# The filler of the sample's attention: two products of each of eight gate pairs in place of two whole pairs

## The chip, the cores and the metric

The kernel runs on one core of a Trainium2 chip. Its time is the device time of one execution in microseconds (us); a measurement runs it several times and takes the median. The core has five engines that work side by side, each through its own list of instructions in a fixed order: TensorE (PE in the profile; its weight loads are PEld), VectorE (DVE), ScalarE (ACT), GpSimd (POOL) and SyncE (SP). SP issues every DMA transfer of this kernel. Engines wait for each other by semaphores. TensorE writes into PSUM, which has eight banks of 128 x 512 fp32 values here; the others read it from there.

## What is computed

One encoder layer, applied to two batches with the same weights: the prompt (512 tokens) and the sample (1024 tokens), 1024 channels each. Cut to what matters:

```python
h = rmsnorm(x, norm_g)
proj = h @ w_in                       # q, k, v, z of two branches; gates ga, gb (1024 wide each)
oa = neighbourhood_attention(qa, ka, va, rpb_a) * silu(za)
ob = window_gqa_attention(qb, kb, vb, t5_table, sink_b) * silu(zb)
merged = sigmoid(ga) * (oa @ w_o_a) + sigmoid(gb) * (ob @ w_o_b)
return x + merged @ w_out
```

The change concerns `ga` and `gb` of the sample: per branch eight blocks of 128 channels (m = 0 to 7), each the product of a 1024 x 128 weight block with h (1024 x 1024 tokens), then a sigmoid.

## The kernel before

**Stages.** The prompt goes first (attention, then the dense phase), then the sample (attention, then the dense phase). In attention, projections (line 761), scores (L934), softmax (L969, L978, L1002 to L1010), transposes (L1026), their split into two parts (L1032, L1037) and the product with v (L1063) alternate. A dense phase is: z pairs (8 blocks of silu(z) times the attention's result), gate pairs (16 blocks of g), the merge (`w_o` products times the sigmoids), and the output projection.

**Precision.** An operand is kept as a high part and a low part (`whi`, `wlo` for weights, `hh`, `hl` for h). `split` (L1163) makes them: ScalarE copies the high part (L1167), VectorE or GpSimd subtracts for the low part (L1172). `product` (L1276) multiplies one 512 x 128 weight block with 512 tokens: 4 steps k of 3 matmuls (L1284 to L1286), 12 matmuls, accumulated in one bank.

**Pairs.** Two neighbouring blocks of channels, two halves of the 1024 input channels and two halves of the tokens form a 2 x 2 by 2 x 2 block product. `pair_classic` makes it with eight products. `pair_strassen` (L1320) makes it with seven: four sums of the weights s1 to s4 (tiles `S`), four sums of h made ahead (`T`), and additions of the results on VectorE (`U`, `C`, L1340 to L1364). Its first two products use no sum at all: product 0 is weight block (0,0) with h block (0,0), product 1 is weight block (0,1) with h block (1,0). Product 0, copied to p1 (L1353), is added to product 1 for the result (0,0), the first channel block's first token half, and it also goes into u2, on which the other results build. Results pass a sigmoid (L1387) and are stored to `g_d` in DRAM (L1394), from where the merge loads them.

**The filler.** `fill_gates` (L1466) makes some gate blocks during attention. Its matmuls have their own weights (`fr` loaded, split to `fh` and `fl`, two buffers each) and their own bank `d`, of which there is one. A finished bank is copied to `fc`, one buffer, by ScalarE or VectorE (L1493), and stored without its sigmoid; the merge then applies the sigmoid in place (L1566). In the sample `FILL_S = 2` makes the last two pairs, branch b's blocks 4 to 7, in this way: per block two token halves, each two products in a row in bank d. The dense phase leaves those pairs out (L1518).

**Order.** All instructions are ordered ahead by a planner, `Flow.run`. It simulates the engines with assumed durations and lags, and gives a free engine the ready operation of the lowest priority number. In the sample's attention the priorities run from 100 to 148; the filler's matmuls and loads have 195, its splits and copies 110 (`soon`), the dense phase 200 and more (a z pair i has 200 + i, a gate pair i 204 + i, the merge 212 + m). So the filler's matmuls go where PE has nothing of attention ready, and its splits and copies ahead of most of attention. The order found is fixed: at run time an engine waits at its next instruction. Weights and tiles rotate through a few buffers, some strictly in turn: `raw` 4, `S` 3, `U` 4, `whi` and `wlo` 6 each of 6 blocks of 128 columns. The first z pair is a classic one; its first two outputs (48 matmuls) need nothing of attention's end, while the sums' products wait until attention's memory is given back (`opened`).

Of the kernel before, what the change touches and what calls it, by code (L numbers as in the profile page):

```python
# [24 lines left out]
ROTA = "ppxxxxxd"  # L25
FILL_P, FILL_S = 3, 2
SLACK = 1.1
# [13 lines left out]
P = 128  # L41
# [313 lines left out]
def encoder_kernel(  # L355
# [780 lines left out]
    def dense_phase(geo, hh, hl, h_ops, o_stores, exps_done, start, opened, tp, up, p0, p1, p2, x_t, y_t, classic, fill, after_gates=None, side=None):  # L1136
# [138 lines left out]

        def product(ps, ws, movs, prio, first, last, after=(), n=nh):  # L1276

            o = None
            for k, ((hi, lo, c, wops), (mh, ml, mops, mv)) in enumerate(zip(ws, movs)):

                def emit(e, k=k, hi=hi, lo=lo, c=c, mh=mh, ml=ml):
                    out = ps.t[:, :n]
                    cs = slice(c, c + P)
                    pe.matmul(out, hi.t[:, cs], mh(), start=first and k == 0, stop=False)  # L1284
                    pe.matmul(out, hi.t[:, cs], ml(), start=False, stop=False)  # L1285
                    pe.matmul(out, lo.t[:, cs], mh(), start=False, stop=last and k == len(ws) - 1)  # L1286
# [32 lines left out]

        def pair_strassen(srcs, post, prio, mov_h, mov_t, seed=None, last=False):  # L1320
            raw = {(m, i): load_raw(srcs[m][i], prio - 2) for m, i in ((0, 0), (1, 0), (1, 1), (0, 1))}
            s1, s2, s3, s4 = (tile_("S", 3, 512) for _ in range(4))
            for out, in0, in1, op in (
# [19 lines left out]
            def result(m, n, x, bank, op=ALU.add):  # L1343
# [122 lines left out]
        def fill_gates(prio):  # L1466


            done = {(k, n): [o for t in range(n * nh // P, (n + 1) * nh // P) for o in h_ops[t]] for k in range(KC) for n in halves}
            mov = blocks(done, nh)  # L1470
            soon = (100 if nt == NT_S else 0) + SOON - f.base
            for br, m in filled:
                his, los = ([f.value(wpool, [P, nh], F32R, tag, 2) for _ in range(2)] for tag in ("fh", "fl"))
                ws = []
                for j in range(2):
                    raw = f.value(wpool, [P, nh], F32, "fr", 2)
                    dma(
                        lambda raw=raw, src=w_g[m, 2 * br + j]: nc.sync.dma_start(raw.t, src), 262144, prio, new=[raw],
                        after=[f.begun[nt, 1 if nt == NT_P else 0]],
                    )  # L1480
                    hi, lo = his[j], los[j]
                    ops = split(
                        lambda hi=hi: hi.t, lambda lo=lo: lo.t, lambda raw=raw: raw.t, nh, soon, (hi, True), (lo, True), [raw],
                    )
                    ws.append([(hi, lo, q * P, ops) for q in range(4)])
                for n in halves:
                    ps = bank("d")
                    o = product(ps, ws[0], mov(0, n), prio, True, False)
                    h_reads.append(product(ps, ws[1], mov(1, n), prio, False, True, [o]))
                    v = f.value(wpool, [P, nh], F32, "fc", 1)  # L1490
                    f.op(
                        (("act", ACT_(nh, False)), ("dve", DVE_(nh))),
                        lambda e, v=v, ps=ps: act.activation(v.t, ps.t, AF.Copy) if e == "act" else dve.tensor_copy(v.t, ps.t),  # L1493
                        soon, new=[v], use=[ps], port=False,
                    )
                    store("g", (br, m, n), g_d[br, m, :, half[n]], v, nh, prio)

# [18 lines left out]
        for i in range(8):  # L1516
            br, m0 = i // 4, 2 * (i % 4)
            if (br, m0) in filled:  # L1518
                if side:
                    side(4 + i)  # L1520
                continue
            srcs = [[w_g[m, 2 * br + j] for j in range(2)] for m in (m0, m0 + 1)]
            post = lambda m, *a, br=br, m0=m0: post_gate(br, m0 + m, *a)
            if i >= 8 - g_classic:
                pair_classic(srcs, post, 4 + i, mov_c)
            else:
                pair_strassen(srcs, post, 4 + i, mov_h, mov_t)
            if side:
# [15 lines left out]
        for m in range(8):  # L1544
# [5 lines left out]
            for n in halves:  # L1550
                gs_ = []
                for br in range(2):
# [219 lines left out]
```

## Time and profile before

| | |
|---|---|
| Median of 3 runs | 1145.79 us (1144.96 to 1147.68) |
| Profiled execution, from the first to the last instruction | 1144.7 us |
| VectorE, ScalarE, GpSimd busy | 854.4, 644.9, 308.3 us |
| Moved by DMA | 159.86 MB, 140 GB/s on average |

The profile is of one execution. Busy time is the union of an engine's instructions; a matmul's row lasts longer than the distance to the next one, because they are pipelined. Rows of the view by stretches name a stretch in us, its length, the busy time of each engine with the number of instructions in brackets, the granted PE clock, the busy share of the DMA engines and GB/s. Rows of the timeline begin with start and duration in us. Rows of the view by tile give the least, median and greatest duration in ns and the first and last start in us. Rows of the view of waits give the sum in us, how often, and the longest. Rows of the groups by line give the count after x, then busy us, mean ns of one, and the idle time before it.

### The profile page before, as it was taken

To read this page: it belongs to the slowest core of one execution; us is meant where nothing else is said; L and a number is where in the kernel's file an instruction comes from. 1 tells how busy PE (TensorE), PEld (TensorE's weight loads), DVE (VectorE), ACT (ScalarE), POOL (GpSimd) and SP (SyncE) were. 2 spreads that over 40 slices of the span, in tenths; PEclk is the share of its full clock that TensorE was granted. 3 is DMA by queue.
4 is the path that set the end of the run, shared out by engine and by line. 5 is a ranking of instruction groups with operands and counts; after the bars stand their busy time and mean duration, and the time that the engine had idled before them with its cause. 6 is when DMAs were issued, how large, how long until landed. Compare 5 with 4: busy or idle time off the path is not lost.

```text
span 1144.7 us, 18482 instructions
## 1 busy us (share of the span) xinstructions
PE 1133.8 (99%) x6139; PEld 985.8 (86%) x6139; DVE 854.4 (75%) x1975; ACT 644.9 (56%) x1467; POOL 308.3 (27%) x413
## 2 busy tenths in 40 slices
PE   8999999999999999999999999999999999999998
PEld 6999988888888899999999888888888888788887
DVE  5888798497765468887778888865878755497984
ACT  5777987544433346665678988865534434343320
POOL 3653433000010054343333445330222210132110
PEclk9999999999999999999999999999999999999999
DMA  7854543488786422121221213226657335573072
GB/s 253 273 158 141 181 113 102 115 264 266 232 277 199 165 72 67 25 70 32 71 61 50 56 37 93 56 66 214 218 148 211 129 111 159 200 238 121 29 223 90
DMA packets 124705, 159.86 MB, mean 140 GB/s; under 512 B 28297, under 2 KB 66961, under 8 KB 124610
## 3 DMA queue, kind: packets, MB, share of 16 engines
q1 hardware_dynamic: 124610, 158.69, 45.4%
q8 instruction: 48, 0.79, 0.3%
q14 instruction: 47, 0.39, 0.1%
HBM read 121.93 MB, written 41.44 MB: 143 GB/s over the span
## 4 chain that ended last, share of the span: by engine, by line
PE 94%; DVE 2%; DMA 2%; ACT 1%; POOL 1%; issue 0%; SPq 0%; ACTq 0%; POOLq 0%
PE p L761 25%; PE x L1285 9%; PE x L1286 9%; PE x L1284 9%; PE x L1063 5%; PE x L1026 5%; PE x L934 4%; PE p L1284 4%; PE p L1285 4%; PE d L1284 4%; PE p L1286 4%; PE d L1286 4%; PE d L1285 4%; PE x L861 2%; DMA ot<-u_d 1%; DMA w<-in_w_att_dram 1%
## 5 line engine op out<-in xcount | busy, mean ns | idle before, releaser
L761 PE MATMUL p<-whi,hh 128*128 128x384 f32 x384 | 133.4, 348 | 0.0
L761 PE MATMUL p<-wlo,hh 128*128 128x384 f32 x384 | 133.1, 347 | 0.0
L761 PE MATMUL p<-whi,hl 128*128 128x384 f32 x384 | 132.4, 345 | 0.0
L978 ACT ACTIVATE sb<-sb,mx 128x384 f32<-128x384 f32 (+1 forms) x192 | 107.5, 563 | 22.4 <-DVE mx L969 22.2
L1167 ACT ACTIVATE whi<-raw 128x512 fp32r<-128x512 f32 (+1 forms) x140 | 81.1, 590 | 52.6 <-PE x L1285 26.2
L761 PE MATMUL p<-whi,hb 128*128 128x384 f32 x384 | 107.5, 347 | 0.0
L1172 POOL TENSOR_TENSOR wlo<-raw,whi 128x512 fp32r<-128x512 f32 (+1 forms) x29 | 40.9, 1413 | 242.4 <-ACT whi L1167 130.4
L1284 PE MATMUL x<-hh,whi 128*128 128x512 f32 x264 | 102.7, 389 | 0.0
L1285 PE MATMUL x<-hl,whi 128*128 128x512 f32 x264 | 102.7, 389 | 0.0
L1286 PE MATMUL x<-hh,wlo 128*128 128x512 f32 x264 | 102.7, 389 | 0.0
L1037 DVE TENSOR_TENSOR pp<-x,pp 128x512 fp32r<-128x512 f32 (+1 forms) x136 | 82.6, 638 | 18.9 <-ACT pp L1032 17.8
L1172 DVE TENSOR_TENSOR wlo<-raw,whi 128x512 fp32r<-128x512 f32 (+1 forms) x111 | 70.1, 645 | 30.5 <-ACT whi L1167 30.2
L1285 PE MATMUL x<-T,whi 128*128 128x512 f32 x224 | 87.5, 390 | 0.3 <-DVE T L1172 0.2
L1286 PE MATMUL x<-T,wlo 128*128 128x512 f32 x224 | 87.2, 389 | 0.0
L1284 PE MATMUL x<-T,whi 128*128 128x512 f32 x224 | 87.1, 389 | 0.0
L1032 ACT ACTIVATE pp<-x 128x512 fp32r<-128x512 f32 (+1 forms) x136 | 70.9, 560 | 22.8 <-PE x L1026 21.8
L799 POOL TENSOR_TENSOR rs_r<-rs_v,mhalf 128x4 f32<-128x4 f32 (+1 forms) x72 | 81.7, 1134 | 5.7
L1063 PE MATMUL x<-pp,v 128*128 128x256 f32 (+1 forms) x368 | 77.8, 324 | 0.8 <-DVE pp L1037 0.8
L792 POOL TENSOR_SCALAR rs_v<-ss 128x4 f32<-128x4 f32 (+1 forms) x72 | 26.2, 364 | 187.3 <-DVE ss L785 184.6
L761 PEld LDWEIGHTS p<-whi,hl 128*128 128x128 f32 x384 | 73.0, 190 | 1.3 <-issue 1.0
L761 PEld LDWEIGHTS p<-wlo,hh 128*128 128x128 f32 x384 | 73.0, 190 | 1.0 <-issue 0.5
L761 PEld LDWEIGHTS p<-whi,hh 128*128 128x128 f32 x384 | 73.0, 190 | 0.9 <-issue 0.5
(351 smaller groups left out, 2985.5 us busy)
## 6 DMA issues: line engine op xcount, KB each, us to landing
raw<-in_w_g_dram SPq DMA_DIRECT2D x76, 256.0 KB
w<-in_w_att_dram SPq DMA_DIRECT2D x46, 384.0 KB
ot<-o_d SPq DMA_DIRECT2D x36, 256.0 KB
g_d<-C SPq DMA_DIRECT2D x34, 256.0 KB
raw<-in_w_z_dram SPq DMA_DIRECT2D x32, 256.0 KB
raw<-in_w_out_dram SPq DMA_DIRECT2D x32, 256.0 KB
C<-g_d SPq DMA_DIRECT2D x24, 256.0 KB
out_dram<-C SPq DMA_DIRECT2D x23, 256.0 KB
```

Source lines behind the costliest of these rows:

```text
L761: pe.matmul(ps.t[:, :GW], part[u](k), mv.t[:, c], start=k == 0 and m == 0, stop=k == KC - 1 and m == 2,)
L799: lambda e: nc.gpsimd.tensor_tensor(r.t[:, :nn], rv.t[:, :nn], mhalf[:, :nn], op=ALU.pow),
L978: act.activation(sb.t[:, :width], sb.t[:, :width], AF.Exp, bias=mx.t[:, i : i + 1], scale=-1.0, accum_out=sm.t[:, i : i + 1],)
L1026: pe.transpose(pt.t[:, u * P : (u + 1) * P], sbs[i].t[:, c * P : (c + 1) * P], ident)
L1032: lambda e, pt=pt, pp=pp, nn=nn: act.activation(pp.t[:, 0, :nn], pt.t[:, :nn], AF.Copy),
L1037: lambda e, pt=pt, pp=pp, nn=nn: dve.tensor_tensor(pp.t[:, 1, :nn], pt.t[:, :nn], pp.t[:, 0, :nn].bitcast(F32), op=ALU.subtract),
L1063: pe.matmul(out(), v.t[:, vs], mv(), start=first, stop=last)
L1167: (("act", ACT_(n)),), lambda e: act.activation(hi(), src(), AF.Copy), prio,
L1172: lambda e: engines[e].tensor_tensor(lo(), src(), hi().bitcast(F32), op=ALU.subtract), prio,
L1284: pe.matmul(out, hi.t[:, cs], mh(), start=first and k == 0, stop=False)
L1285: pe.matmul(out, hi.t[:, cs], ml(), start=False, stop=False)
L1286: pe.matmul(out, lo.t[:, cs], mh(), start=False, stop=last and k == len(ws) - 1)
```

## The change

For the sample, all eight gate pairs now have a part in the filler (`FILL_S` is 8). Of each pair only the first channel block (`filled[::2]`) and only the two products without sums are made there: product 0 in bank d, whose copy is kept in DRAM (`p_d`) while the bank is not cleared; then, after that copy, product 1 on top of it in the same bank, whose copy is the result (0,0) and goes to `g_d`. The dense phase then makes every gate pair with five products; it loads product 0 into p1 instead of computing it, and neither makes nor stores the result (0,0). The merge applies its in-place sigmoid to the results (0,0) alone. The sums of weights, h and results are as before. The prompt takes none of this (`short`).

```diff
-FILL_P, FILL_S = 3, 2
+FILL_P, FILL_S = 3, 8
...
+        p_d = None if short else dpool.tile([2, 4, P, sn], F32, tag="p_d", name="p_d")
...
-        def pair_strassen(srcs, post, prio, mov_h, mov_t, seed=None, last=False):
+        def pair_strassen(srcs, post, prio, mov_h, mov_t, seed=None, last=False, kept=None):
...
-            w = weight_tiles([raw[0, 0], raw[0, 1], s2, s3, s1, raw[1, 1], s4], 6, prio - 0.5)
+            first = [] if kept else [raw[0, 0], raw[0, 1]]
+            w = weight_tiles([*first, s2, s3, s1, raw[1, 1], s4], 6, prio - 0.5)
+            w = [None] * (7 - len(w)) + w
...
-            a = mul(0, mov_h(0, 0))
-            f.op(
-                (("act", ACT_(sn)),), lambda e: act.activation(p1.t, a.t[:, :sn], AF.Copy), prio, new=[p1], use=[a]
-            )
-            result(0, 0, p1, mul(1, mov_h(1, 0)))
+            if kept:
+                src, after = kept
+                dma(lambda: nc.sync.dma_start(p1.t[:, :sn], src), 512 * sn, prio - 0.5, new=[p1], after=after)
+            else:
+                a = mul(0, mov_h(0, 0))
+                f.op(
+                    (("act", ACT_(sn)),), lambda e: act.activation(p1.t, a.t[:, :sn], AF.Copy), prio, new=[p1], use=[a]
+                )
+                result(0, 0, p1, mul(1, mov_h(1, 0)))
...
-            for br, m in filled:
+            for br, m in filled if short else filled[::2]:
...
-                for n in halves:
-                    ps = bank("d")
-                    o = product(ps, ws[0], mov(0, n), prio, True, False)
-                    h_reads.append(product(ps, ws[1], mov(1, n), prio, False, True, [o]))
...
+                for n in halves if short else (0,):
+                    ps = bank("d")
+                    o = product(ps, ws[0], mov(0, n), prio, True, not short)
+                    if not short:
+                        o = leave(ps, "p", (br, m), p_d[br, m // 2])
+                    h_reads.append(product(ps, ws[1], mov(1, n), prio, False, True, [o], again=not short))
+                    leave(ps, "g", (br, m, n), g_d[br, m, :, half[n]])
...
-            if (br, m0) in filled:
+            if (br, m0) in filled and short:
...
+                kept = (p_d[br, m0 // 2], stores["p", br, m0]) if (br, m0) in filled else None
+                pair_strassen(srcs, post, 4 + i, mov_h, mov_t, kept=kept)
...
-                    if (br, m) in filled:
+                    if (br, m) in filled and (short or (m % 2, n) == (0, 0)):
                         sigmoid(g, nh, prio, True)
```

`leave` is the copy to `fc` and the store, formerly written out in the loop. `again` tells the program's builder that the second product goes on in a bank whose group was closed.

More of the change, by code (lines that the diff above doesn't have):

```diff
@@ L1274, in weight_tiles, with product @@
             return out
-        def product(ps, ws, movs, prio, first, last, after=(), n=nh):
+        def product(ps, ws, movs, prio, first, last, after=(), n=nh, again=False):
             o = None
@@ L1283, in emit @@
                     cs = slice(c, c + P)
-                    pe.matmul(out, hi.t[:, cs], mh(), start=first and k == 0, stop=False)
-                    pe.matmul(out, hi.t[:, cs], ml(), start=False, stop=False)
-                    pe.matmul(out, lo.t[:, cs], mh(), start=False, stop=last and k == len(ws) - 1)
+                    more = {"skip_group_check": True} if again else {}
+                    pe.matmul(out, hi.t[:, cs], mh(), start=first and k == 0, stop=False, **more)
+                    pe.matmul(out, hi.t[:, cs], ml(), start=False, stop=False, **more)
+                    pe.matmul(out, lo.t[:, cs], mh(), start=False, stop=last and k == len(ws) - 1, **more)
                 kw = {"new": [ps]} if first and k == 0 else {"into": [ps]}
@@ L1485, in fill_gates, with leave @@
                     ws.append([(hi, lo, q * P, ops) for q in range(4)])
-                for n in halves:
-                    ps = bank("d")
-                    o = product(ps, ws[0], mov(0, n), prio, True, False)
-                    h_reads.append(product(ps, ws[1], mov(1, n), prio, False, True, [o]))
+                def leave(ps, kind, key, dst):
                     v = f.value(wpool, [P, nh], F32, "fc", 1)
-                    f.op(
+                    o = f.op(
                         (("act", ACT_(nh, False)), ("dve", DVE_(nh))),
@@ L1495, in fill_gates @@
                     )
-                    store("g", (br, m, n), g_d[br, m, :, half[n]], v, nh, prio)
+                    store(kind, key, dst, v, nh, prio)
+                    return o
+                for n in halves if short else (0,):
[5 more added lines that the diff above has]
+                    leave(ps, "g", (br, m, n), g_d[br, m, :, half[n]])
         filled = [(i // 4, 2 * (i % 4) + j) for i in range(8 - fill, 8) for j in range(2)]
```

1 line of the change is left out of this document (removed).

## The prediction

> **What bounds the kernel now.** I read the page first: engine shares and the chain that ended last.
>
> ```profile
> span 1144.7 us, 18482 instructions
> ...
> PE 1133.8 (99%) x6139; PEld 985.8 (86%) x6139; DVE 854.4 (75%) x1975; ACT 644.9 (56%) x1467; POOL 308.3 (27%) x413
> ...
> PE 94%; DVE 2%; DMA 2%; ACT 1%; POOL 1%; issue 0%; SPq 0%; ACTq 0%; POOLq 0%
> ```
>
> TensorE (PE) is busy 99% of the span and makes 94% of the chain. An average says nothing about a stage, so next comes the view by stretches, cut at the sample's stages: attention (384 to 782), z pairs (to 858), gate pairs (858 to 972), merge (972 to 1060).
>
> ```profile
> core 0: us, PE busy (x) PEld busy (x) DVE busy (x) ACT busy (x) POOL busy (x), PEclk, DMA share, GB/s
> 384.00:600.00 216.00, 215.19 (x1401) 202.72 (x1401) 165.93 (x485) 130.09 (x346) 79.05 (x114) 1.00 0.24 70
> 600.00:740.00 140.00, 139.21 (x889) 124.07 (x886) 119.64 (x323) 119.97 (x285) 61.15 (x91) 1.00 0.23 56
> 740.00:777.00 37.00, 37.00 (x212) 30.52 (x211) 26.35 (x72) 23.75 (x66) 10.89 (x18) 1.00 0.29 70
> 777.00:790.00 13.00, 13.00 (x62) 10.80 (x62) 5.41 (x9) 5.96 (x10) 0.00 (x0) 1.00 0.46 128
> 790.00:858.00 68.00, 68.00 (x301) 56.31 (x300) 52.55 (x84) 31.03 (x61) 13.34 (x9) 1.00 0.68 214
> 858.00:972.00 114.00, 114.00 (x504) 94.40 (x503) 76.35 (x115) 47.60 (x89) 17.22 (x11) 1.00 0.48 152
> 972.00:1060.00 88.00, 87.66 (x385) 71.71 (x385) 64.10 (x91) 32.99 (x56) 19.05 (x13) 1.00 0.57 186
> ```
>
> PE has no hole above a microsecond in any stage; in the gate stage 504 matmuls take 114.00 us, 0.226 us each. Busy time can hide small stalls, so the spacing of starts is the test:
>
> ```profile
> 791.39 0.39 PE L1284 MATMUL x<-hh,whi 128*128 128x512 f32 x1
> 791.61 0.39 PE L1285 MATMUL x<-hl,whi 128*128 128x512 f32 x1
> 791.84 0.39 PE L1286 MATMUL x<-hh,wlo 128*128 128x512 f32 x1
> 792.07 0.39 PE L1284 MATMUL x<-hh,whi 128*128 128x512 f32 x1
> ```
>
> A row lasts 0.39 but the next starts 0.227 later: back to back, and the z stage (301 in 68.00) and the gate stage keep the same distance. So a 512-column matmul costs 0.226 us of the span wherever PE is fed. The Trainium skill ("Perfetto Trace Analysis", Identifying the Most-Contended Engine) calls matmul busy time a bad measure and prefers the share of LDWEIGHTS, which is 94.40 of 114.00 here (83%) and would leave PE room; by it the gate stage is not PE's and the change gives nothing (third rival). The trace does not agree: the spacing is even at its least. By the skill's warm gap for 512 columns ("TensorE: Matmul & The Clock Gate", Back-to-back issue gap, about 216 ns) an estimate of the 24 matmuls below would be 5.2 us instead of 5.4.
>
> **The change, part by part.**
>
> *Matmuls.* Only the sample's part changes. Before: the filler makes 4 gate channels, each 2 halves x 2 products x 4 k x 3 = 48 matmuls, 192 in all; six gate pairs of seven products (84 matmuls) make 504: together 696. After: eight filler items of two products (24), again 192; eight pairs of five products (60) make 480: together 672. **24 matmuls of 512 columns go, all from the gate stage: 24 x 0.226 = 5.4 us.** The filler's volume, and so PE's work in attention, stays.
>
> *The filler's new wait.* Line 1284 of an item's second product now follows a copy of the same bank (line 1493), so PE gets 12 matmuls at a time instead of 24 before it must wait, and 16 copies instead of 8 go through the one `fc` buffer. Where the filler runs now:
>
> ```profile
> 384.00:600.00 216.00, 7.11 (x26) 4.40 (x24) 0.69 (x1) 0.60 (x1) 1.00 0.24 70
> 600.00:700.00 100.00, 15.36 (x57) 10.37 (x57) 0.69 (x1) 0.60 (x1) 1.00 0.22 55
> 700.00:740.00 40.00, 6.92 (x27) 5.10 (x28) 0.67 (x1) 0.00 (x0) 1.00 0.25 60
> 740.00:777.00 37.00, 21.29 (x83) 15.05 (x84) 1.38 (x2) 0.60 (x1) 1.00 0.29 70
> ```
>
> These are bank d's instructions alone: 26 matmuls in the first 216 us, 84 in the next 140, 83 in the last 37. Until 740 it is thin and between other PE work; it is dense only in the tail. There, today's boundary between two groups is this:
>
> ```profile
> 758.03 0.39 PE L1286 MATMUL d<-hh,fl 128*128 128x512 f32 x1
> 758.35 1.33 PE L934 MATMUL x<-kt,q 64*128 64x384 f32 x12
> 759.61 0.50 PE L1284 MATMUL d<-hh,fh 128*128 128x512 f32 x1
> 759.94 0.40 PE L1285 MATMUL d<-hl,fh 128*128 128x512 f32 x1
> ```
>
> The bank rests 1.2 us for its copy and a score batch fills it. All PE waits of attention are these three, none on bank d:
>
> ```profile
> PE x L1063 <- DVE pp L1037: 0.8, 2, 0.6
> PE x L861 <- DVE qk L816: 0.5, 1, 0.5
> PE x L1026 <- DVE sb L1010: 0.3, 1, 0.3
> ```
>
> So eight existing boundaries of the same kind cost nothing visible. Behind a waiting matmul stands all of PE, since it runs in its written order; what the planner writes into the gap is the cover: attention's own work, and from 747 on the first z pair, whose matmuls already run as filler after the last item:
>
> ```profile
> 777.29 0.39 PE L1284 MATMUL p<-hh,whi 128*128 128x512 f32 x1
> ...
> 781.59 1.10 PE L1063 MATMUL x<-pp,v 128*128 128x512 f32 x4
> ```
>
> The batch at 781.59 is attention's last on PE. 48 of that pair's matmuls need nothing of attention's end; three ran at 747 and some 15 from 777.29 to 781.59, so about 30 were still unused (6.8 us of PE work). Filler that slides past attention's end is not lost either. Bounds for eight new boundaries: 0 (as the present ones) to 8 x 1.2 = 9.6 us (none covered). I take 0.8: a fresh start after other work costs about 0.1 (759.61 to 759.94 is 0.33 against 0.227) times eight, near the lower end, to which the rows are nearer.
>
> *VectorE and ScalarE in attention.* Eight more weight halves are split, eight more copies made:
>
> ```profile
> L1167 ACT ACTIVATE fh<-fr x8: 625/632/638, 397.9 to 758.2; 128x512 fp32r<-128x512 f32 x8
> L1172 DVE TENSOR_TENSOR fl<-fr,fh x8: 684/692/739, 398.6 to 759.1; 128x512 fp32r<-128x512 f32 x8
> ```
> ```profile
> L1493 ACT ACTIVATE fc<-d x4: 598/599/601, 597.0 to 777.5; 128x512 f32<-128x512 f32 x4
> ...
> L1493 DVE COPY fc<-d x4: 670/692/692, 678.2 to 758.5; 128x512 f32<-128x512 f32 x4
> ```
>
> ScalarE gets 8 x 0.632 and, at the present half share, 4 x 0.599: 7.5 us. VectorE gets 12 x 0.692: 8.3 us. They stand ahead of later attention work in priority (110). Both engines are 85 to 86% busy from 600 to 740, so the additions fit their idle time, but attention's chain may stretch. PE then runs filler and z work instead. I cost it at nothing beyond the 0.8; uncovered it would be up to 8.3.
>
> *Gate stage.* A pair falls from 84 to 60 matmuls, 19.0 to 13.6 us, and keeps its four weight sums, so the other engines have less time for each:
>
> ```profile
> L1172 DVE TENSOR_TENSOR wlo<-S,whi 128x512 fp32r<-128x512 f32 (+1 forms) x26 | 16.9, 667 | 4.2 <-ACT whi L1167 3.9
> L1161 DVE TENSOR_TENSOR C<-U,x 128x512 f32<-128x512 f32 x16 | 10.9, 682 | 6.1 <-PE x L1286 6.0
> ```
>
> VectorE now spends 76.35 / 6 = 12.7 us on a pair (z's last work included); two splits and one result go, 3 x 0.68, leaving 10.7 of 13.6 (79%). ScalarE spends 47.60 / 6 = 7.9; two splits, one copy and one sigmoid go (0.6 each, as the split and the copy above), leaving 5.5. The z stage ran VectorE at 52.55 of 68 (77%) with PE at 68.00 of 68: the cover holds. Transfers: eight 256 KB raw loads, eight loads of the kept product more; results stored stay 24. That is 4.2 MB in a stage shortened to 109 us: 152 x 114 / 109 + 39 = 198 GB/s, below the z stage's 214 at a full PE. SP's single queue issues these 16 more; attention gets 16 more too (weights, kept products), some 10 GB/s on 56 to 70. A pair's weights now fill four of the six weight buffers, formerly five, so the planner can prepare about a pair ahead. Cost: nothing; without cover, the shortfall is that of the 5.4.
>
> *Merge.* Eight in-place sigmoids before, eight after, at other m; ScalarE is 38% busy there. Nothing.
>
> **Sum.** Against the profiled execution: 1144.7 - 5.4 + 0.8 = 1140.1. The runs' median, 1145.8, lies 1.1 above that span; so 1145.8 - 4.6 = **1141.2 us**.
>
> **The rivals.**
>
> *The copies are uncovered.* PE waits 1.2 us at several new boundaries; with three to seven uncovered 3.6 to 8.4 is lost, so about 1144 to 1149. For it: the planner takes its own durations for granted and PE cannot pass a late copy, and between 600 and 740 there is no z work yet. Against: no PE wait on bank d today. 12%, two thirds of it within 0.2% of before.
>
> *The softmax engines become attention's bound* (the other side). The 110-priority splits and copies delay scores and exponentials where ScalarE and VectorE are at 86%; all 8.3 us appear as PE idle: 1145.8 - 5.4 + 8.3 = 1148.7. It makes the kernel slower from 5.4 us on. Against: 30 spare z matmuls cover 6.8 of it. 6%.
>
> *The gate stage stops being PE's.* VectorE or the raw loads take 14.3 us or more for a pair (8 x 14.3 = 114), or PE never bound this stage: 1145.8, no change. Against: 10.7 us of VectorE, and the even spacing. 5%; partial forms near 1143.
>
> *PE slows after pauses.* The trace shows it once, after its idle start: 18 instructions in one 5 us, 32 in another, both at a granted clock of 1.00.
>
> ```profile
> 11.00:16.00 5.00, 5.00 (x18) 4.90 (x17) 4.23 (x8) 2.49 (x5) 0.37 (x1) 1.00 0.91 319
> 17.00:22.00 5.00, 5.00 (x32) 4.97 (x31) 2.41 (x6) 3.47 (x8) 1.71 (x4) 1.00 1.01 373
> ```
>
> One such stretch costs 5 x (1 - 18/32) = 2.2 us; eight would be 17.5, giving about 1158. The new pauses are 1.2 us at most, and today's show nothing of the kind: 1%. The Trainium skill ("TensorE: Matmul & The Clock Gate", A second HAM failure mode) states the rule: cycling one PSUM queue lets PE idle often enough to lose its clock; the gap at 758 kept a spacing near 0.23, so the trace does not bear it out.
>
> *It doesn't do what it says:* the filler doesn't fit attention and runs after it. The matmul count is the same, hence 1140 to 1142: no separate result; 2%, counted with the forecast.
>
> **How the numbers follow.** About 0.2% (2.3 us) can be told from no change. Forecast and fitting filler 76%, all faster. Uncovered copies: 8% same, 4% slower. Softmax engines: 1% same, 5% slower. Gate stage: 2% faster, 3% same. Clock 1% slower. That gives 0.78, 0.12, 0.10. The range starts at the full 5.4 with the merge's hole of 0.34 us (87.66 of 88) gone as well, less the 0.8 by which the runs scatter below their median, and reaches up into the uncovered copies and the half-bound gate stage: 1139.2 to 1145.2.
>
> **What would show it.** Right: 24 fewer 512-column matmuls on PE; a gate stage near 109 us with the spacing still 0.226; attention's last batch still near 782; no PE wait on an `fc` copy. Wrong: PE waits in attention of over 2 us together, on `fc` copies (first rival) or on L1037 and L1010 (second); PE waits in the gate stage on VectorE or a DMA (third).

## The result, and the profile after

| | before | changed | ratio, 95% interval |
|---|---|---|---|
| Median of 5 runs | 1145.79 us (1144.96 to 1148.53) | 1142.48 us (1140.72 to 1145.24) | 0.9965 [0.995, 0.998] |
| The profiled execution: span | 1144.7 us | 1143.4 us | |

The kernel became faster, by 4.0 us (2.3 to 5.7) where 4.6 was forecast. The profiled execution of the changed kernel is the slowest of its five runs, so its span must not be subtracted from that of before; the stages show what belongs to the change. The head of its page:

```profile
span 1143.4 us, 18577 instructions
...
PE 1129.6 (99%) x6115; PEld 981.9 (86%) x6115; DVE 858.3 (75%) x1994; ACT 645.1 (56%) x1477; POOL 319.4 (28%) x420
...
PE 92%; DMA 3%; DVE 2%; ACT 1%; POOL 1%; issue 1%; SPq 0%; POOLq 0%; DVEq 0%; ACTq 0%
```

6139 - 6115: the 24 matmuls are gone. The view by stretches follows, cut at the same six matmuls in both kernels: the sample's first projection, its 97th, the 49th matmul of the first z pair, and the first matmul of the gate pairs, the merge and the output projection. The changed kernel:

```profile
397.40:417.20 19.80, 18.44 (x106) 17.61 (x105) 11.59 (x29) 7.67 (x17) 6.94 (x9) 1.00 0.50 160
417.20:793.50 376.30, 374.55 (x2402) 340.58 (x2401) 305.37 (x871) 271.59 (x696) 141.32 (x203) 1.00 0.25 68
793.50:861.50 68.00, 68.00 (x301) 56.31 (x300) 54.08 (x86) 32.14 (x61) 14.75 (x11) 1.00 0.75 234
861.50:970.30 108.80, 108.80 (x481) 90.09 (x480) 74.56 (x117) 44.74 (x86) 27.53 (x24) 1.00 0.59 188
970.30:1058.41 88.11, 87.74 (x385) 71.91 (x384) 63.59 (x89) 31.51 (x55) 21.28 (x15) 1.00 0.57 186
```

The kernel before, at the same marks:

```profile
395.13:413.88 18.75, 18.23 (x106) 17.69 (x105) 11.02 (x29) 7.66 (x17) 6.63 (x9) 1.00 0.52 170
413.88:789.35 375.47, 374.38 (x2403) 340.66 (x2401) 301.16 (x852) 268.35 (x683) 144.46 (x212) 1.00 0.22 58
...
857.35:971.59 114.24, 114.24 (x506) 94.59 (x504) 76.53 (x116) 47.83 (x88) 17.22 (x11) 1.00 0.48 152
971.59:1059.71 88.12, 87.78 (x385) 71.84 (x384) 63.81 (x91) 32.91 (x56) 18.77 (x13) 1.00 0.57 187
```

The second number of a row is the length. The gate stage lost 114.24 - 108.80 = 5.44 us, and PE fills all of it. The second row, which I call **the rest of attention**, holds the same matmuls in both kernels and became 0.83 us longer. PE's idle time in it (length less PE busy) went from 375.47 - 374.38 = 1.09 to 376.30 - 374.55 = 1.75 us. The z stage did not move. The sample begins 2.27 us later (397.40 against 395.13), before anything that the change touches. The waits of PE in the changed kernel say where that came from:

```profile
PE x L861 <- DVE qk L816: 3.1, 5, 1.0
PE x L1026 <- DVE sb L1010: 2.3, 2, 2.0
PE d L1286 <- ACT fc L1498: 0.2, 1, 0.2
```

The single wait of 2.0 us on `sb` lies in the prompt. In the repeat e1 (below) it is missing:

```profile
PE x L1026 <- DVE sb L1010: 0.3, 1, 0.3
```

So the time of this one profile is 2 us of the prompt's scatter and a start of the sample's attention that is 1.05 us longer (19.80 against 18.75; the repeats gave 19.59 and 18.64), laid over a change of -5.44 + 0.83.

### The profile page after: what moved, and what is told of

It reads as the page before. It is cut to its first block, busy times and chain, and to the rows that moved or that the text cites. A ratio compares the mean times of both kernels' runs of the same rounds, so it can differ in the third digit from the quotient of the medians.

```text
span 1143.4 us, 18577 instructions
## 1 busy us (share of the span) xinstructions
PE 1129.6 (99%) x6115; PEld 981.9 (86%) x6115; DVE 858.3 (75%) x1994; ACT 645.1 (56%) x1477; POOL 319.4 (28%) x420
## 4 chain that ended last, share of the span: by engine, by line
PE 92%; DMA 3%; DVE 2%; ACT 1%; POOL 1%; issue 1%; SPq 0%; POOLq 0%; DVEq 0%; ACTq 0%
PE p L761 23%; PE x L1288 10%; PE x L1287 10%; PE x L1286 10%; PE x L1063 5%; PE x L1026 5%; PE x L934 5%; PE p L1287 4%; PE p L1286 4%; PE p L1288 4%; PE d L1286 4%; PE d L1288 4%; PE d L1287 4%; PE x L861 2%; DMA w<-in_w_att_dram 1%
## 5 line engine op out<-in xcount | busy, mean ns | idle before, releaser
L1168 ACT ACTIVATE whi<-raw 128x512 fp32r<-128x512 f32 (+1 forms) x124 | 73.8, 607 | 60.2 <-PE x L1287 29.5
L1287 PE MATMUL x<-T,whi 128*128 128x512 f32 x256 | 99.7, 390 | 0.2 <-DVE T L1173 0.2
L1286 PE MATMUL x<-T,whi 128*128 128x512 f32 x256 | 99.7, 389 | 0.0
L1288 PE MATMUL x<-T,wlo 128*128 128x512 f32 x256 | 99.6, 389 | 0.0
L1037 DVE TENSOR_TENSOR pp<-x,pp 128x512 fp32r<-128x512 f32 (+1 forms) x136 | 82.6, 638 | 20.8 <-ACT pp L1032 19.7
L1288 PE MATMUL x<-hh,wlo 128*128 128x512 f32 (+1 forms) x232 | 89.8, 387 | 0.0
L1287 PE MATMUL x<-hl,whi 128*128 128x512 f32 (+1 forms) x232 | 89.8, 387 | 0.0
L1286 PE MATMUL x<-hh,whi 128*128 128x512 f32 (+1 forms) x232 | 89.8, 387 | 0.0
L1173 POOL TENSOR_TENSOR wlo<-raw,whi 128x512 fp32r<-128x512 f32 (+1 forms) x27 | 35.6, 1323 | 182.7 <-ACT whi L1168 182.6
L1173 DVE TENSOR_TENSOR wlo<-raw,whi 128x512 fp32r<-128x512 f32 (+1 forms) x97 | 65.3, 680 | 25.8 <-ACT whi L1168 25.4
```

Source lines behind the costliest of these rows:

```text
L1037: lambda e, pt=pt, pp=pp, nn=nn: dve.tensor_tensor(pp.t[:, 1, :nn], pt.t[:, :nn], pp.t[:, 0, :nn].bitcast(F32), op=ALU.subtract),
L1168: (("act", ACT_(n)),), lambda e: act.activation(hi(), src(), AF.Copy), prio,
L1173: lambda e: engines[e].tensor_tensor(lo(), src(), hi().bitcast(F32), op=ALU.subtract), prio,
L1287: pe.matmul(out, hi.t[:, cs], ml(), start=False, stop=False, **more)
```

## The experiments

In the table, "rest" is the rest of attention and "busy" PE's busy time in it, both read from the rows of the view by stretches as above, as are gate stage and merge. "Before beside it" is the median of the kernel before on the same chip; the ratio is to that. Times in us.

| run | median | before beside it | ratio, 95% interval | rest | busy | gates | merge |
|---|---|---|---|---|---|---|---|
| before (profile above) | 1145.79 | | | 375.47 | 374.38 | 114.24 | 88.12 |
| changed (profile above) | 1142.48 | 1145.79 | 0.9965 [0.995, 0.998] | 376.30 | 374.55 | 108.80 | 88.11 |
| e1_repeat | 1141.27 | 1146.83 | 0.9961 [0.9947, 0.9974] | 376.42 | 374.53 | 108.80 | 89.21 |
| e11_after_third | 1141.74 | 1146.38 | 0.9964 [0.9951, 0.9978] | 376.42 | 374.68 | 108.80 | 88.62 |
| e2_drop24 | 1139.74 | 1146.83 | 0.9946 [0.9934, 0.9959] | 375.45 | 374.36 | 108.80 | 87.58 |
| e3_add24 | 1147.33 | 1146.83 | 1.0004 [0.9994, 1.0015] | 376.22 | 374.54 | 114.24 | 88.90 |
| e4_nowait | 1142.04 | 1146.83 | 0.9966 [0.9955, 0.9977] | 377.23 | 375.30 | 108.80 | 88.71 |
| e5_sharew | 1138.74 | 1146.20 | 0.9937 [0.9923, 0.995] | 374.20 | 373.90 | 108.80 | 87.75 |
| e6_both | 1140.59 | 1146.20 | 0.9953 [0.9937, 0.997] | 375.46 | 374.37 | 108.80 | 87.77 |
| e7_late | 1140.29 | 1146.20 | 0.9948 [0.9934, 0.9962] | 375.75 | 374.37 | 108.80 | 88.50 |
| e12_late_again | 1140.04 | 1146.38 | 0.9945 [0.9932, 0.9957] | 375.74 | 374.37 | 108.81 | 88.86 |
| e9_splitlate | 1140.65 | 1146.38 | 0.9946 [0.9934, 0.9959] | 375.21 | 374.23 | 108.80 | 88.59 |
| e10_copylate | 1140.80 | 1146.38 | 0.995 [0.9938, 0.9963] | 375.64 | 374.52 | 108.80 | 87.94 |
| e8_nmajor | 1148.09 | 1146.20 | 1.002 [1.0011, 1.003] | 376.45 | 374.67 | 108.80 | 87.81 |

### The same kernel again

No edit. The expectations of both runs:

> The changed kernel once more, for a second profile. In the first profile the sample's attention began 2.27 us later than in the profile of before (397.40 against 395.13), all of it from one stall of 2 us at 69 us in the prompt, which the change does not touch; attention then lost 1.9 us and the gates gained 5.4. If that stall is scatter of one execution, the sample's attention begins within 0.3 us of 395.1 here, the span is near 1141.2 (1144.7 - 5.4 + 1.9), and the ratio to before is 0.995 to 0.998. Rival: the changed program itself delays the prompt; then the 2.3 us are there again.

> The changed kernel a third time, beside e9, e10 and e12 on one chip: a median 3.5 to 4.6 us below the kernel before; the rest of attention again 376.3 to 376.5 us, the gate stage 108.8. If the rest moves by more than 0.2, a term of 0.9 us cannot be read from single profiles and what e4 to e7 said of it falls.

In e1 the sample's attention began at 393.09 us, 2 us ahead of the expected 395.1: the 2 us wait was scatter, but the profile of before is no fixed mark either, and the prompt moves by some 2 us each way. Three comparisons give 4.0, 4.5 and 4.1 us (0.0035, 0.0039 and 0.0036 of the time before). The rest of attention came out as 376.30, 376.42 and 376.42: the +0.83 to +0.95 is real and repeats to 0.12 us, although whole runs scatter by three or four microseconds. So that row, and not the median, is what the smaller experiments are read from. e2 leaves attention as it was and gives 375.45 beside 375.47, which says the same of the kernel before.

### The gate stage alone

e2 is the kernel before with the four `wlo` matmuls left out of the seventh product of each of the six gate pairs; e3 is the changed kernel with three more matmuls in the third product of each of its eight gate pairs:

```diff
# e2_drop24, in product (thin is a new argument of it)
-                    pe.matmul(out, hi.t[:, cs], ml(), start=False, stop=False)
-                    pe.matmul(out, lo.t[:, cs], mh(), start=False, stop=last and k == len(ws) - 1)
+                    pe.matmul(out, hi.t[:, cs], ml(), start=False, stop=thin and last and k == len(ws) - 1)
+                    if not thin:
+                        pe.matmul(out, lo.t[:, cs], mh(), start=False, stop=last and k == len(ws) - 1)
...
-                h_reads.append(product(ps, w[i], mov, prio, True, True, [opened], sn))
+                h_reads.append(product(ps, w[i], mov, prio, True, True, [opened], sn, i == 6 and not short and not seed and prio >= 4))
# e3_add24, in mul
-                h_reads.append(product(ps, w[i], mov, prio, True, True, [opened], sn))
+                wi = w[i]
+                if kept and i == 2:
+                    wi, mov = [*wi, wi[3]], [*mov, mov[3]]
+                h_reads.append(product(ps, wi, mov, prio, True, True, [opened], sn))
```

> The kernel before with 24 matmuls less in its gate stage and nothing else: in the seventh product of each of six gate pairs the four matmuls with the low part of the weights are left out, all copies, sums, splits and transfers stay. Theory (the gate stage is bound by PE): the gate stage shortens by 24 x 0.2267 = 5.4 us, attention stays as before, about 1140.4 us, ratio 0.9953. Rival (another engine or the transfers bind the gate stage in part): clearly less than 5.4, ratio above 0.997.

> The changed kernel with its 24 saved matmuls given back: the third product of each of the eight gate pairs does one of its four k steps twice (3 matmuls more per pair). What is left is the change's cost in attention alone. Theory: attention costs 0.8 to 1.9 us, so 1146.6 to 1147.7 us, ratio 1.0007 to 1.0017 (same). Rival (attention costs nothing and the gates gave less than 5.4): 1145.8 or less.

Gate stage of e2, then of e3:

```profile
855.91:964.71 108.80, 108.80 (x482) 90.13 (x480) 73.11 (x115) 46.85 (x86) 15.16 (x10) 1.00 0.48 150
```

```profile
856.60:970.84 114.24, 114.24 (x506) 94.65 (x504) 73.35 (x116) 45.29 (x86) 25.68 (x24) 1.00 0.54 178
```

The stage's length is its matmuls times 0.2267, whichever kernel they stand in; the loads, sums and stores around them do not count. With its 24 matmuls given back the changed kernel is where the kernel before is: +0.5 us (-0.7 to +1.7), below the expected 0.8 to 1.9, but the interval holds most of that, and zero; the row of its rest (+0.75) decides more than its median. And 24 matmuls fewer without any new filler are worth 6.2 us by the medians (4.7 to 7.6; 5.44 of it is in the gate stage), of which the changed kernel keeps 4.0 to 4.5.

### Copies and splits in attention: one at a time, then both

What costs the 0.9 us? (A bank is the 128 x 512 block in which PE adds up a product. No GpSimd row of the profile before reads one; VectorE and ScalarE do, and the filler's copies go to these two.) Per filler item, the change adds a copy with a wait between two products, and it splits every weight for one use instead of two. e4 takes the first away, e5 the second for half the items, e6 both:

```diff
# e4_nowait (the last argument, twin, is a second place to store to)
...
-                    o = product(ps, ws[0], mov(0, n), prio, True, not short)
-                    if not short:
-                        o = leave(ps, "p", (br, m), p_d[br, m // 2])
-                    h_reads.append(product(ps, ws[1], mov(1, n), prio, False, True, [o], again=not short))
-                    leave(ps, "g", (br, m, n), g_d[br, m, :, half[n]])
+                    o = product(ps, ws[0], mov(0, n), prio, True, False)
+                    h_reads.append(product(ps, ws[1], mov(1, n), prio, False, True, [o]))
+                    leave(ps, "g", (br, m, n), g_d[br, m, :, half[n]], None if short else p_d[br, m // 2])
# e5_sharew: nothing loaded or split for every second item
...
+                old = not short and m % 4 == 2
+                if not old:
...
-                for j in range(2):
+                for j in () if old else range(2):
```

> The changed kernel without the copy between an item's two products: the 24 matmuls run through as before the change, the finished bank is copied once and this copy is stored to both places, so the kept product holds the sum of the two. Eight copies and eight waits of the filler are gone, the doubled weight splits stay. Theory A (the copies and the waits for them cost attention its 0.8 to 1.9 us): attention is that much shorter than in the changed kernel, about 1141 us. Theory B (the splits ahead of the softmax cost it): attention as in the changed kernel, 1142.5 us. Theory C (scatter): no difference to e1 beyond 0.5 us in attention's length.

> The changed kernel with half of the filler's weight splits: every second item takes the weights of the item before it, so eight loads and sixteen splits (eight on ScalarE, eight on VectorE or GpSimd) fall out of attention; copies and waits stay. Counted without the first 25 us, where a late mask load scatters, the sample's attention took 0.9 us longer in three profiles with the change's filler than in two with the filler of before. If the splits ahead of the softmax cause it, that part falls by 0.5 us or more here; if the copies or mere reordering do, it stays within 0.3 us of the changed kernel's. Time 1141 to 1143 us either way.

> Both at once: one copy for an item's two products (no wait between them) and shared weights, so ScalarE and VectorE do for the filler what they did before the change, while gates and merge are as changed. If the filler's added work costs attention its 0.9 us, attention without its first 25 us is back within 0.3 us of the kernel before; if that length is only a matter of which order the planner happens to find, it stays 0.5 us or more above. Time about 1141.5 us.

The rest of attention, in e4, e5 and e6:

```profile
411.82:789.05 377.23, 375.30 (x2403) 340.56 (x2401) 304.55 (x855) 274.48 (x698) 145.01 (x211) 1.00 0.25 70
```

```profile
412.94:787.14 374.20, 373.90 (x2402) 340.65 (x2401) 300.85 (x856) 273.79 (x697) 139.22 (x208) 1.00 0.23 65
```

```profile
413.33:788.79 375.46, 374.37 (x2403) 340.67 (x2401) 301.62 (x853) 268.05 (x683) 143.10 (x211) 1.00 0.24 64
```

Without the copy the rest is *longer*, by 0.8 to 0.9 us, which none of the three theories had: taking the new wait out gains nothing. With half the splits it is 2.1 to 2.2 shorter, and PE idles 0.30 us in it where the kernel before idled 1.09; the median, 1138.74, is below the 1141 to 1143 expected. With both edits the rest is that of before to 0.01. I read from this that the doubled splits cost about 2 us, since they go ahead of the softmax's work, and that the shorter items give about 1 back. Read as a price of each kind of instruction, that theory forecasts what priorities alone should do, and so it was tested.

One thing stands against that reading already. In e6 the matmuls of the rest come in exactly the order of the kernel before, and its waits of PE there are the same, to the line:

```profile
PE x L1063 <- DVE pp L1037: 0.8, 2, 0.6
PE x L1026 <- DVE sb L1010: 0.3, 1, 0.3
```

So e6 is no sum of two effects. The planner found the old order again, and 375.47, 375.45 (e2) and 375.46 are three measurements of one order.

### Priorities alone: where the theory fell

The changed kernel, with splits and copies (e7, e12), the splits only (e9) or the copies only (e10) given priority 140 instead of 110 in the sample's attention; no work is added or removed:

```diff
# e7_late and e12_late_again
-            soon = (100 if nt == NT_S else 0) + SOON - f.base
+            soon = (100 + 30 if nt == NT_S else 0) + SOON - f.base
# e9_splitlate: in the filler's split
-                        lambda hi=hi: hi.t, lambda lo=lo: lo.t, lambda raw=raw: raw.t, nh, soon, (hi, True), (lo, True), [raw],
+                        lambda hi=hi: hi.t, lambda lo=lo: lo.t, lambda raw=raw: raw.t, nh, soon + (0 if short else 30), (hi, True), (lo, True), [raw],
# e10_copylate: in leave
-                        soon, new=[v], use=[ps], port=False,
+                        soon + (0 if short else 30), new=[v], use=[ps], port=False,
```

> The changed kernel with the filler's splits and copies at priority 140 instead of 110, behind the softmax of nearly all of attention. If their place ahead of the softmax costs attention its 0.9 us, it gets shorter by 0.5 us or more, about 1141.5 us; if PE needs the filler where it is now, PE waits grow between 600 and 780 and the time rises by 1 us or more.

> The changed kernel with one edit: the filler's weight splits have priority 140 instead of 110 in the sample's attention; the copies out of bank d keep 110. The part of attention from the 97th projection matmul to the 49th dense one ('the rest') took 376.30 and 376.42 us in the changed kernel, 375.46 before, 374.20 with every second split left out, 377.23 without the copy between the products, 375.75 with splits and copies both at 140. Theory (the doubled splits, ahead of the softmax's work, cost about 2 us; the copies and the wait behind them give about 1 back): moving only the splits behind gives at least what e7 gave, the rest 374.5 to 375.8, the span 1 to 2 us below the changed kernel's. Rival (the copies at 110 are the cost, and e7 gained by moving them): the rest stays at 376.3 or more, and e10 has the gain. Second rival (the planner's order changes with any edit and the rest scatters by half a microsecond either way, with no cause in splits or copies): e7's 375.75 lies between e9 and e10, or both are above it.

> The changed kernel with the other edit: the copies out of bank d have priority 140, the splits keep 110. Theory (splits cost, copies do not): the rest of attention is 376.0 us or more, no better than the changed kernel's 376.36. Rival (the copies at 110 are the cost): 375.75 or less, as in e7. Second rival (any new order gives a new rest within half a microsecond): anything from 375.8 to 376.9, without relation to e9.

> Splits and copies both at 140 (e7) again, beside the changed kernel on one chip. Theory: the rest of attention is 375.7 to 375.8 again, and the median is 0.3 to 1.5 us below e11's. Rival (e7's lower median, 1140.29 against 1141.27 and 1142.48, was scatter of the prompt and the merge): the rest may repeat, but the medians of e11 and e12 agree within 0.3 us or turn round.

The rest of attention in e9, then in e10:

```profile
413.17:788.38 375.21, 374.23 (x2402) 340.55 (x2400) 303.37 (x869) 276.48 (x701) 137.18 (x198) 1.00 0.25 68
```

```profile
414.16:789.80 375.64, 374.52 (x2403) 340.71 (x2401) 306.69 (x861) 275.37 (x696) 143.82 (x215) 1.00 0.25 69
```

e9 came out where the theory put it (375.21; 374.5 to 375.8). e10 did not: 375.64 instead of 376.0 or more. Its rival, that the copies alone are the cost, falls with e9. And the parts do not add up: -1.2 for the splits, -0.8 for the copies, but -0.7 for both together (375.75). So there is no price per split or per copy; moving either takes most of the 0.9 away. What is left is the second rival, that each edit gives a new order with a rest of its own. Its signs as written did not come (375.64 is below its 375.8, and 375.75 lies above both e9 and e10), and the orders span 3 us instead of half a microsecond. But no order scatters like that when it is run again: e12 repeats e7 to 0.01, and the five profiles with the changed kernel's order in attention (changed, e1, e3, e8, e11) lie within 376.22 to 376.45. So the difference lies in each order itself.

**What the rests are made of.** A few waits of PE in each. The changed kernel's from 415 to 795 us, then e5's, then e9's (of the kernel before: the two lines above):

```profile
PE x L861 <- DVE qk L816: 1.2, 2, 1.0
PE x L1026 <- DVE sb L1010: 0.3, 1, 0.3
PE d L1286 <- ACT fc L1498: 0.2, 1, 0.2
```

```profile
PE x L1026 <- DVE sb L1010: 0.3, 1, 0.3
```

```profile
PE d L1286 <- ACT fc L1498: 0.7, 1, 0.7
PE x L1026 <- DVE sb L1010: 0.3, 1, 0.3
```

These sums are the idle times (rest less busy) of 1.75, 0.30 and 0.98. Idle time leaves out the first part of each wait, because a row lasts longer than the distance to the next start; so I took the distances themselves, and counted by how much single ones exceed what the same matmul, behind and ahead of the same kinds, takes elsewhere in the traces (0.2 us and more, without the one on `sb` that all share). The kernel before has two, 0.76 and 0.35 us, both on `pp`. The changed kernel has three: 1.17 and 0.39 on `qk`, 0.38 on `fc`. That is +1.94 and -1.11, together the whole +0.83. Without such starts 374.36 us are left in both kernels, and 374.20 to 374.50 in every profile but e4's. Yet PE goes from other work into the filler 43 times in the changed kernel and 33 times before: ten more starts, at no cost of their own.

**What holds the longest.** The order is fixed, so its stalls must be in each profile of it. The waits of 0.8 us on `pp` that PE had before are gone; the longest one now, 1.0 us (1.17 by the starts), is new. PE in the changed kernel there, by the timeline:

```profile
552.05 0.34 PE L761 MATMUL p<-whi,hl 128*128 128x384 f32 x1
553.39 0.41 PE L861 MATMUL x<-ident,qk 128*128 128x128 f32 x2 [1.00 <-DVE qk L816]
```

VectorE, which makes that `qk`, in the same timeline:

```profile
550.01 0.42 DVE L1076 TENSOR_TENSOR ot__7028<-ot__7028 64x256 f32<-64x256 f32 x1 [0.65 <-ACT ot__7028 L1070]
550.35 0.68 DVE L1498 COPY fc<-d 128x512 f32<-128x512 f32 x1
551.06 1.85 DVE L1080 TENSOR_TENSOR ot__7028<-ot__7028 64x256 f32<-64x256 f32 x1
552.83 0.41 DVE L816 TENSOR_TENSOR qk<-p,rs_r 128x256 f32<-128x256 f32 x1
```

GpSimd:

```profile
550.78 3.81 POOL L607 TENSOR_TENSOR wlo<-w,whi 128x768 fp32r<-128x768 f32 x2 [0.26 <-ACT whi L602]
```

Its two subtractions by line, with the least, median and greatest duration and both starts:

```profile
L607 POOL TENSOR_TENSOR wlo<-w,whi x2: 1841/1923/2005, 550.8 to 552.6; 128x768 fp32r<-128x768 f32 x2
```

The addition of line 1080 takes 1.85 us, and lasts until GpSimd's first subtraction (1.84 from 550.78, so to 552.62) is over. In the kernel before the like of it lasts 0.42, and VectorE itself makes that subtraction:

```profile
545.10 0.42 DVE L1080 TENSOR_TENSOR ot__6998<-ot__6998 64x256 f32<-64x256 f32 x1
545.45 0.28 DVE L809 TENSOR_TENSOR v<-p,v 128x128 fp32r<-128x128 f32 x1
545.65 0.94 DVE L607 TENSOR_TENSOR wlo<-w,whi 128x768 fp32r<-128x768 f32 x1
```

The filler's copy (0.68) stands ahead of line 1080 in VectorE's queue. Without it, line 1080 would have followed line 1076 at about 550.4, ahead of GpSimd's start at 550.78. Coming second, it ends after GpSimd does, and `qk` and PE wait behind it: it is 1.43 us late, more than the 1.17 that PE lost. The same piece in the repeat e1:

```profile
545.94 0.68 DVE L1498 COPY fc<-d 128x512 f32<-128x512 f32 x1
546.64 1.86 DVE L1080 TENSOR_TENSOR ot__7028<-ot__7028 64x256 f32<-64x256 f32 x1
```

All five profiles with this order (changed, e1, e3, e8, e11) have one L1080 of 1.85 to 1.86 us; in the nine others none exceeds 0.61. The Trainium skill states this rule ("SBUF — State Buffer", Who interferes with whom): an instruction of VectorE with two inputs from SBUF and one of GpSimd that reads SBUF exclude each other, and the later one is blocked until the other has ended. The trace agrees: 0.42 becomes 1.85, and the end lies 0.3 us behind GpSimd's. That this one meeting makes the 1.17 is argued from the profiles; no run took it out alone, and what makes the second wait on `qk` is open. Other orders have other waits: in e7, e9 and e10 most or all of them stand behind the filler's own late copies, and e4, free of the meeting, has the longest rest, with these:

```profile
PE x L1026 <- DVE sb L1010: 0.8, 2, 0.5
PE d L1286 <- ACT fc L1498: 0.6, 1, 0.6
PE x L1026 <- DVE mx L969: 0.5, 1, 0.5
```

By the starts they are 0.74, 0.71 and 0.66 us. That leaves 375.12, some 0.8 above the others, and e4's PE busy time, with the same matmuls, is 0.9 above that of before: several more late starts of 0.1 to 0.2 us, which longer rows cover, make part of it. The remainder is open.

Leaving aside e2, e5 and e6, which drop work, e7 and e12 are the fastest: 1140.29 and 1140.04, in their comparisons 6.0 and 6.3 us below the kernel before. Beside e12 on one chip the changed kernel (e11) took 1.7 us more, and each of its five runs (1141.62 to 1143.73) is longer than each of e12's (1139.24 to 1141.40); 0.3 to 1.5 was expected. By the profiles 0.7 of it is in the rest of attention, and repeats; e12's sample also began 1.3 us earlier, which the edit does not touch. e7 ran beside no changed kernel.

### The merge

In e8 the loop that loads the four inputs of the merge's h sums takes the halves outside and the blocks inside, to see whether the hole at the merge's start comes from the order of those loads:

```diff
-            for c in range(8):
-                for n in halves:
+            for n in halves:
+                for c in range(8):
```

> The changed kernel with one loop turned: at the start of the merge the 16 loads of the attention branch go through all channel blocks of the first token half and then of the second, formerly both halves of each block. Four profiles with the changed gate stage have a merge of 88.1 to 89.2 us against 87.6 and 88.1 with the old one; 384 matmuls at 0.2267 are 87.05. Theory: PE waits there for loads that come one by one through two buffers, seven before the first product is complete; with four the merge falls to 87.1 to 87.6 us and the kernel to about 1141 us. Rival: the wait is for the weight sums' tiles to come free, then the merge stays at 88 to 89 us.

Inconclusive on the merge: 87.81 is above the 87.1 to 87.6 of the theory, below the 88 of the rival, and lies within what kernels that were not edited there show (87.58 to 89.21). The kernel became slower instead of reaching 1141 us, 1148.09, by a loss of its own, in the output projection:

```profile
PE x L1288 <- DVE wlo L1173: 5.1, 1, 5.1
```

So the merge stays open: the kernels with the old gate pairs (before, e2) have 88.12 and 87.58, the three profiles of the changed one 88.11, 89.21 and 88.62. That would be up to 0.8 us in the mean, but single values overlap.

## Why the prediction was right, and where it was not

**The time and its sign.** 1141.2 was forecast; the medians are 1142.48, and 1141.27 and 1141.74 in the repeats, all inside the range of 1139.2 to 1145.2 and all faster by more than 0.2%.

**24 x 0.226 = 5.4 us, all from the gate stage: right.** 5.44 in each profile, and e2 and e3 take it away and give it back. The even spacing of starts was the right test; the share of weight loads (83% before, 90.09 of 108.80 after, the same) would have promised PE room that isn't there.

**The gate stage's cover: right.** PE fills 108.80 of 108.80. VectorE spends 74.56 / 8 = 9.3 us on a pair (10.7 was worked out; GpSimd took over part, 24 instructions in 27.53 us for 11 in 17.22), ScalarE 44.74 / 8 = 5.6 (5.5), and the transfers run at 188 GB/s (198).

**"I take 0.8", for eight fresh starts: right in size, wrong in its cause.** This is the step that failed. A start after other work is no cost of its own: with ten more of them the rest without its late starts is 374.36 us, as before. What attention did lose, 0.83 to 0.95 us, is three waits of PE that are new (1.94 in the first profile) less two that went away (1.11), and the longest stands behind a block on VectorE that the prediction did not look for. e4 fits: without the eight boundaries attention gets longer, not shorter. That the sum came out right is luck: the new waits less the old ones happened to be about as long as the term that wasn't there.

**"I cost it at nothing beyond the 0.8", for VectorE and ScalarE: mis-sized.** All three new waits are for VectorE or ScalarE. What the splits and copies cost there is not their length (8.3 us if uncovered) but where they fall in the order: giving them another place is worth 0.7 to 1.2 us (e7, e9, e10), and the order that the planner finds with half of the splits has none of these waits and is 2.2 shorter (e5).

**The filler slides, as worked out.** Its last copy now begins at 785.3, formerly at 777.5; counted from the 97th projection (417.20 and 413.88) that is 4.5 us later. Attention's last batch on PE, at 786.44 and 781.59, is 1.5 later by the same count. The copies of the changed kernel, by tile:

```profile
L1498 ACT ACTIVATE fc<-d x9: 597/599/608, 496.2 to 785.3; 128x512 f32<-128x512 f32 x9
...
L1498 DVE COPY fc<-d x7: 675/691/692, 550.4 to 772.2; 128x512 f32<-128x512 f32 x7
```

Yet, counted from the 97th projection, the 49th z matmul is only 0.8 to 1.0 us later than before: z matmuls did take the place that the filler left.

**Merge, nothing: open** (0 to 0.8 us). Its hole of 0.34 did not go either (88.11 - 87.74 = 0.37), so the range's lower end had a gain too many.

**The rivals.** Uncovered copies: PE waits on `fc` once, for 0.2 us (0.38 by the starts). Softmax engines: the mechanism is there in small, 0.7 us more idle time and not 8.3. Its sign, waits of PE of over 2 us on L1037 and L1010, did not come (0.3 on L1010 in the rest); in their place PE waits on `qk` L816, 1.4 us in attention's first 16 us and 1.2 in the rest. Gate stage not PE's: refuted by e2 and e3. PE slowing after the new pauses: it did not, the projections start 0.17 us apart again behind the wait of 1.0 us, and a filler step of 512 columns 0.23 apart behind the one on `fc`. (The granted clock of 1.00 that the prediction reads beside its slow stretch is no measurement: that trace has no clock record ahead of 16.15 us. The distances, 0.32 us there and 0.17 later for the same 384 columns, are.)

## What to carry to other kernels

Where starts of matmuls follow each other evenly in a stage, matmuls taken out of it count in full, and the rows of that stage show it to a hundredth of a microsecond while medians scatter by microseconds. In a kernel whose order is fixed, filler work costs little through its matmuls; it costs through single waits that its splits and copies make in the queues of other engines. There the order matters more than the amount, so list the waits of the order first, and try priorities before removing work. An edit that changes the order is not a price of what it removes: compare the orders before adding effects up. When a sum comes out right, still test its terms: here one right total hid a term that was not there.

## What the runs showed that was not expected

**A short addition blocked for 1.4 us by GpSimd.** Line 1080 in 1.85 instead of 0.42 us, shown above: moving a 768-column subtraction from VectorE (0.94) to GpSimd (1.84) isn't free for VectorE while it adds two SBUF operands. Such blocks are common and mostly free: in the gate stage of the kernel before, seven VectorE rows behind the start of a GpSimd row last 1.42 to 1.78 us instead of 0.68, and PE fills 114.24 of 114.24. This one cost because PE stood behind it.

**A pause of 5 us does slow PE, one of 1 us doesn't.** Around the 5.05 us wait in e8's output projection (DVE wlo, above), three stretches of 5 us:

```profile
1078.00:1083.00 5.00, 0.59 (x3) 0.17 (x1) 5.00 (x10) 1.26 (x2) 1.26 (x1) 0.82 0.19 74
1083.00:1088.00 5.00, 4.35 (x10) 3.47 (x11) 2.49 (x4) 0.63 (x1) 0.00 (x0) 0.50 0.97 296
1088.00:1093.00 5.00, 5.00 (x23) 4.11 (x22) 3.05 (x6) 1.00 (x3) 0.00 (x0) 1.00 0.91 305
```

In the second one PE still waits for 0.65 us, then makes 10 matmuls in 4.35 us at a granted clock of 0.50, 0.43 us apart; in the third it makes 23 again. The output projection took 92.39 us instead of 85.03, 7.4 more for a wait of 5.1: some 2.3 for the slow stretch, near the 2.2 that the prediction worked out for one. The Trainium skill ("TensorE: Matmul & The Clock Gate", What's actually happening) puts the limit at an idle window of about 3.4 us. The trace has the clock fall sooner: a mean of 0.82 in the first row, if the clock is either 1.00 or 0.50 in it, means 1.8 us at 0.50, so from about 1081.2 on, and PE's last row ahead of the wait ended at 1078.6, 2.6 us before. After the 1.0 us wait in attention there is no loss.
